# Down projection of a transformer block: all block sums moved from GpSimd to VectorE, the seven products in another order

## The chip, the cores and the metric

One core of one Trainium2 chip. The metric is the device time of one execution in microseconds (us); each kernel is executed several times and the median counts. A profile is one further execution, recorded instruction by instruction.

## What is computed

One layer of a hybrid block over 16 learned tokens and 1024 frames, everything in float32: a combined projection, attention and pooling side by side, an output projection, and then the part that matters here, the gated feed-forward:

```python
n2 = _rmsnorm(h, norm2_w)
ffn = (jax.nn.silu(n2 @ w_gate) * (n2 @ w_up)) @ w_down     # D_MODEL 1024, D_FF 2816
return h + ffn                                              # the 16 learned tokens are dropped at the end
```

The change touches the last product alone, `(...) @ w_down`, with the sum `h + ffn` behind it.

## The kernel before

The kernel runs in stages one after the other: input projections, attention, output projection, gate and up products, down projection. A list written out by hand, not a scheduler, sets the order on each engine: each engine executes its instructions in the order of the program, and waits where an operand or a buffer isn't ready.

**The down projection** is one matrix product: 1024 output rows by 1024 frames, summed over 2816 hidden rows. Hidden rows are stored as 22 tiles of 128 rows, `hid[0..21]`, read back from DRAM; even tiles are called `ha`, odd ones `hc`. The product is done with a scheme of seven block products in place of eight (Strassen's, in Winograd's form): the weights are cut into 2x2 blocks (even or odd hidden tile by lower or upper 512 output rows, `LO` and `HI`), the hidden values into 2x2 blocks (even or odd tile by lower or upper 512 frames). Each of the seven products `j` multiplies one block, or a sum of blocks, of the weights with one block, or a sum, of the hidden values. The outputs are sums of products. `SEQD` (L990) is the order of the products, 1, 2, 4, 6, 7, 5, 3.

**One product** has 11 steps `i` (`NPR`, one for each pair of hidden tiles), so the down projection has 77 steps, numbered x. A step has a weight tile `wd` and a hidden tile `hd`. float32 is multiplied as a rounded part and a remainder, both in a faster format: the tile's lower half holds the rounded values, the upper half the remainders. For each of four output tiles `m` a step issues three matmuls of 128x128 by 128x512 (L1362 to L1364): 12 a step, 132 a product, 924 in all. The four outputs of a product are four PSUM banks; two products' banks fit.

**What a step needs first**, in `d_prep` (L1022):
- the block sum of the weights and that of the hidden values, where the product has one: L1032, L1035, L1041, L1046, L1050, L1054 and L1062 on GpSimd (`G`), L1036 and L1042 on VectorE (`V`);
- for `wd` and then for `hd`: ScalarE casts the values to the rounded part (L1058), VectorE subtracts it from the values to get the remainder (L1059).

So a step's chain is sum, cast, remainder, matmul. `d_ahead(x)` runs ahead of the matmuls of step x: it issues hidden loads up to step x + `HL`, weight loads up to x + `LL` and `d_prep` up to x + `LS` = x + 2 (L1065). All loads are on SyncE's queue (SP), which issues in order.

**The evacuation** `d_evac` (L1330) takes the outputs of a product out of PSUM: one bank m after each of the next product's first four steps, always behind that step's `d_ahead`. Product 1 and product 4 are copied by ScalarE, the others are added by VectorE, straight from PSUM, into `dx`, `du` or `res` tiles (all by the helper at L1325, so they share a line); GpSimd adds `dp` and `du` for one output block (also L1325). `res_load` (L1316) fetches the residual h, which GpSimd adds at step 6 of products 2, 6, 5 and 3. `give` stores a finished output block from ScalarE's queue. In the last product the last three steps (`TL`) are done output by output, so that outputs finish one after the other.

**Buffers**: `ut` tiles (41 of 128x1024) hold the hidden tiles, `wd`, `hd`, `dx`, `du`, `dp` and the stored sums `T2d` and `S2d`; `hs` (10 of 128x512) hold 512-column weights and residuals; `aux` (3 of 128x1024) the wider weight loads.

Of the kernel before, what the change touches and what calls it, by code (L numbers as in the profile page):

```python
# [7 lines left out]
FT = mybir.dt.float32  # L8
FR = mybir.dt.float32r
AF = mybir.ActivationFunctionType  # L10
OP = mybir.AluOpType
# [20 lines left out]
NB = (3, 6)  # L32
CW, KW, SW, W1 = 2, 2, 3, 3
TL = 3
HL, LL, LS = 8, 4, 2
LA = 3
MAXN = {0: (2, 0, 0), 1: (0, 2, 2, 2, 2, 2, 2)}
SUBV = 4
# [7 lines left out]
def block_kernel(ctx, tc, hT, n1w, w_f, w_v, w_u, w_qk, b_f, qnw, knw, w_pool, pscale, w_out, n2w, w_g, w_up, w_d, outT):  # L46
# [12 lines left out]
    def ut(cols, dt=FT, s="u"):  # L59
        return U.tile([128, cols], dt, tag="u", bufs=NU, padded_shape=None, name=nm(s))  # L60
# [14 lines left out]
    V, A, G = nc.vector, nc.scalar, nc.gpsimd  # L75
# [55 lines left out]
    def load(src, cols, mk, eng=None):  # L131
        t = mk(cols, FT, "wst")
        (eng or nc.sync).dma_start(t, src)
        return t

    def aux(cols, dt=FT, s="ax"):
        return U.tile([128, cols], dt, tag="aux", bufs=NAUX, name=nm(s))
# [849 lines left out]

    SEQD = (1, 2, 4, 6, 7, 5, 3)  # L990
    dseq = [(j, i) for j in SEQD for i in range(NPR)]
    horder = [2 * i for i in range(NPR)] + [2 * i + 1 for i in range(NPR)]
    hid, T2d, S2d, wraw, dparts = {}, {}, {}, {}, {}
    dnext = [0, 0, 0]
    LO, HI = slice(0, 512), slice(512, 1024)

# [5 lines left out]

    def d_load(j, i):
        e, o = w_d[2 * i], w_d[2 * i + 1]
        if j in (1, 2, 4, 3):
            return load({1: e[:, LO], 2: o[:, LO], 4: o[:, HI], 3: o[:, LO]}[j], 512, hs)
        if j == 6:
            return load(e, 1024, aux), load(o[:, HI], 512, hs)
        if j == 7:
            return load(e, 1024, aux)  # L1010
        t = aux(1024, FT, "wst")
        nc.sync.dma_start(t[:, LO], e[:, HI])  # L1012
        nc.sync.dma_start(t[:, HI], o[:, HI])
        return t

    def halves(store, i, s):

        if i % 2 == 0:
            store[i // 2] = ut(1024, FT, s)
        return store[i // 2][:, 512 * (i % 2):512 * (i % 2) + 512]  # L1020

    def d_prep(j, i):  # L1022
        w = wraw.pop((j, i))
        ha, hc = hid[2 * i], hid.get(2 * i + 1)

        def t2():
            return T2d[i // 2][:, 512 * (i % 2):512 * (i % 2) + 512]
        if j == 1:
            b = ha[:, LO]
        elif j == 2:  # L1030
            b = hc[:, LO]
            G.tensor_tensor(halves(T2d, i, "T2d"), hc[:, HI], ha[:, LO], op=OP.subtract)  # L1032
        elif j == 4:
            b = hc[:, LO]
            G.tensor_tensor(b, b, t2(), op=OP.subtract)  # L1035
            V.tensor_tensor(ha[:, HI], hc[:, HI], ha[:, HI], op=OP.subtract)  # L1036
        elif j == 6:
            b = t2()
            w, c = w
            s2 = halves(S2d, i, "S2d")  # L1040
            G.tensor_tensor(c, c, w[:, HI], op=OP.add)  # L1041
            V.tensor_tensor(s2, c, w[:, LO], op=OP.subtract)  # L1042
            w = s2
        elif j == 7:
            b = ha[:, HI]
            G.tensor_tensor(w[:, LO], w[:, LO], w[:, HI], op=OP.subtract)  # L1046
            w = w[:, LO]
        elif j == 5:
            b = ha[:, LO]
            G.tensor_tensor(w[:, LO], w[:, LO], w[:, HI], op=OP.add)  # L1050
            w = w[:, LO]
        else:
            b = hc[:, HI]
            G.tensor_tensor(w, w, S2d[i // 2][:, 512 * (i % 2):512 * (i % 2) + 512], op=OP.subtract)  # L1054
        out = []
        for src, name in ((w, "wd"), (b, "hd")):
            t = ut(1024, FR, name)
            A.activation(t[:, LO], src, AF.Copy)  # L1058
            V.tensor_tensor(t[:, HI], src, f(t)[:, LO], op=OP.subtract)  # L1059
            out.append(t)  # L1060
        if j == 1:
            G.tensor_tensor(ha[:, LO], ha[:, HI], ha[:, LO], op=OP.subtract)  # L1062
        dparts[j, i] = out

    def d_ahead(x):  # L1065
# [242 lines left out]
    stores()  # L1308


    ux, uu, up4, todo = [ut(1024, FT, "dx") for _ in range(2)], [], [], []

    def of(ts, m):
        return ts[m // 2][:, 512 * (m % 2):512 * (m % 2) + 512]

    def res_load(r, b):  # L1316
        out = []
        for m in range(4):
            t = hs(512, FT, "res")
            nc.sync.dma_start(t, h2d[4 * r + m][:, 512 * b:512 * b + 512])  # L1320
            out.append(t)
        return out

    def add(e, out, p, q):
        e.tensor_tensor(out, p, q, op=OP.add)  # L1325

    def give(r, b, m, t):
        todo.append(lambda: A.dma_start(outT[4 * r + m][:, 512 * b:512 * b + 512], t))

    def d_evac(j, m, p):  # L1330
        x = of(ux, m)
        if j == 1:
            A.activation(x, p, AF.Copy)
        elif j == 2:
            t = res.pop(0)
            add(V, t, p, t)
            give(0, 0, m, t)
        elif j == 4:
            A.activation(of(up4, m), p, AF.Copy)
        elif j == 6:  # L1340
            add(V, x, p, x)
        elif j == 7:
            u, t = of(uu, m), of(up4, m)
            add(V, u, p, x)
            add(G, t, t, u)
            give(1, 0, m, t)
        elif j == 5:
            t = res.pop(0)
            add(V, t, p, t)
            add(V, x, p, x)  # L1350
            give(1, 1, m, t)


    RES = {2: (0, 0, lambda m: of(ux, m)), 6: (1, 0, lambda m: of(up4, m)), 5: (1, 1, lambda m: of(uu, m)),
           3: (0, 1, lambda m: of(ux, m))}
    res, done = [], []

    def part(j, steps, m, p):
# [5 lines left out]
            mm(p, w[:, W], h[:, HI], start=False, stop=i == NPR - 1)  # L1364

    for y, j in enumerate(SEQD):
        if j == 4:
            up4.extend(ut(1024, FT, "dp4") for _ in range(2))
        if j == 7:
            uu.extend(ut(1024, FT, "du") for _ in range(2))  # L1370
        pb = [ps("d") for _ in range(4)]
        tl = TL if j == SEQD[-1] else 0
        for i in range(NPR - tl):
            d_ahead(NPR * y + i)
            for m in range(4):
                part(j, (i,), m, pb[m])
            dparts.pop((j, i))
            while todo:
                todo.pop(0)()
            if done:  # L1380
                d_evac(*done.pop(0))
            elif j in RES and i == 4:
                r, b, with_ = RES[j]
                res.extend(res_load(r, b))
            elif j in RES and i == 6:
                for m in range(4):
                    t = RES[j][2](m)
                    if j == 6:
                        add(G, t, t, res.pop(0))
                    else:  # L1390
                        add(G, res[m], res[m], t)
        if not tl:
            done.extend((j, m, pb[m]) for m in range(4))
    d_ahead(len(dseq) - 1)
# [1 line left out]
        todo.pop(0)()  # L1396
    for m in range(4):
        part(j, range(NPR - tl, NPR), m, pb[m])
        t = res.pop(0)
        add(V, t, pb[m], t)  # L1400
        A.dma_start(outT[m][:, HI], t)

# [51 lines left out]
```

## Time and profile before

| | us |
|---|---|
| median of 3 runs | 1186.5 (1186.46 to 1186.7) |
| profiled execution, its own time | 1182.54 |
| its span, first to last instruction | 1180.8 |
| TensorE busy in the span | 1131.0 (96%) |
| VectorE busy | 786.7 (67%) |
| GpSimd busy | 566.8 (48%) |
| ScalarE busy | 483.7 (41%) |

The profiled execution is 4.0 us under the median of the runs, and 1.7 us over its own span. "Busy" counts an instruction from its start to its end; matmuls follow each other before the one in front has ended, so a busy TensorE can still run slowly, and how fast it runs is read from the distance of two matmuls' starts. The granted clock is given as a share of TensorE's full 2.4 GHz.

### The profile page before, as it was taken

How to read it: one execution, taken by the hardware profiler on the slowest of the kernel's cores; microseconds unless marked ns; L12 is line 12 of the kernel's file. 1: busy time of each engine (PE TensorE's matmuls, PEld its weight loads, DVE VectorE, ACT ScalarE, POOL GpSimd, SP SyncE). 2: the span in 40 equal slices, each digit the busy share in tenths (PEclk: the TensorE clock that was granted, in tenths of full speed). 3: DMA queues.
4: the chain of work that ended last, by engine and by line, in shares of the span. 5: the costliest groups of instructions: out<-in, count | busy, mean ns of one | idle time of the engine just before them, and what ended most of it. 6: DMA issues, size and time to landing. Idle time of an engine off the chain costs nothing. (4 is left out here: it accounts for less than half of the span.)

```text
span 1180.8 us, 14713 instructions
## 1 busy us (share of the span) xinstructions
PE 1131.0 (96%) x5251; PEld 922.5 (78%) x5251; DVE 786.7 (67%) x1144; ACT 483.7 (41%) x903; POOL 566.8 (48%) x433
## 2 busy tenths in 40 slices
PE   6899999999999999898999999999999998999988
PEld 5787999787888878676888888888888886767766
DVE  7524753774888877899455545544555599988587
ACT  7333421532788775434333123322332362334332
POOL 6200235142446574647435533453345389465493
PEclk9899999999999999998999999999999999999989
DMA  6201110251021131221223221323132692566554
GB/s 218 72 1 54 36 54 10 64 162 45 19 48 34 29 110 75 100 79 57 82 76 105 74 84 59 107 72 102 42 107 74 240 372 72 180 222 195 171 170 132
DMA packets 49993, 118.23 MB, mean 100 GB/s; under 512 B 6736, under 2 KB 9296, under 8 KB 49920
## 3 DMA queue, kind: packets, MB, share of 16 engines
q1 hardware_dynamic: 40096, 101.00, 26.2%
q10 hardware_dynamic: 9824, 16.30, 3.7%
q8 instruction: 41, 0.67, 0.2%
q14 instruction: 32, 0.26, 0.1%
HBM read 91.86 MB, written 19.92 MB: 95 GB/s over the span
## 5 line engine op out<-in xcount | busy, mean ns | idle before, releaser
L1124 PE MATMUL gu<-cb,ws 128*128 128x512 f32 x560 | 221.7, 396 | 4.1 <-DVE ws L1114 4.1
L1125 PE MATMUL gu<-cb,ws 128*128 128x512 f32 x560 | 221.6, 396 | 0.0
L1123 PE MATMUL gu<-cb,ws 128*128 128x512 f32 x560 | 221.2, 395 | 0.0
L1114 DVE TENSOR_TENSOR ws<-wst,ws 128x512 fp32r<-128x512 f32 x120 | 97.2, 810 | 125.1 <-ACT ws L1113 125.0
L1364 PE MATMUL d<-hd,wd 128*128 128x512 f32 x308 | 125.9, 409 | 8.2 <-DVE hd L1059 7.6
L1124 PEld LDWEIGHTS gu<-cb,ws 128*128 128x128 f32 x560 | 105.8, 189 | 29.6 <-DVE ws L1114 4.5
L1362 PE MATMUL d<-hd,wd 128*128 128x512 f32 x308 | 123.8, 402 | 4.0 <-ACT hd L1058 3.9
L1113 ACT ACTIVATE ws<-wst 128x512 fp32r<-128x512 f32 x120 | 69.9, 621 | 138.8 <-POOL wst L1108 130.9
L1125 PEld LDWEIGHTS gu<-cb,ws 128*128 128x128 f32 x560 | 105.9, 189 | 24.6
L1363 PE MATMUL d<-hd,wd 128*128 128x512 f32 x308 | 123.8, 402 | 1.4 <-DVE wd L1059 1.3
L1123 PEld LDWEIGHTS gu<-cb,ws 128*128 128x128 f32 x560 | 105.7, 189 | 24.7
L1137 POOL TENSOR_TENSOR e<-e,e 128x512 f32<-128x512 f32 x20 | 29.6, 1478 | 159.5 <-DVE e L1150 99.8
L1059 DVE TENSOR_TENSOR wd<-wst,wd 128x512 fp32r<-128x512 f32 x66 | 70.2, 1063 | 25.6 <-ACT wd L1058 25.5
L1058 ACT ACTIVATE wd<-wst 128x512 fp32r<-128x512 f32 x66 | 41.6, 630 | 108.5 <-POOL wst L1050 27.8
L293 POOL TENSOR_TENSOR s<-t,g 128x346 f32<-128x346 f32 (+2 forms) x20 | 21.5, 1081 | 131.9 <-ACT g L292 121.2
L1059 DVE TENSOR_TENSOR hd<-wst,hd 128x512 fp32r<-128x512 f32 x66 | 84.6, 1282 | 0.0
L736 POOL TENSOR_TENSOR pl<-p,ph 128x512 fp32r<-128x512 f32 (+4 forms) x58 | 64.8, 1130 | 41.1 <-ACT p L728 38.5
L1364 PEld LDWEIGHTS d<-hd,wd 128*128 128x128 f32 x308 | 59.1, 192 | 29.6 <-DVE hd L1059 16.8
L1362 PEld LDWEIGHTS d<-hd,wd 128*128 128x128 f32 x308 | 59.3, 192 | 18.3 <-ACT hd L1058 5.7
L402 PE MATMUL pj<-xh,wl 128*128 128x346 f32 (+2 forms) x216 | 72.9, 338 | 0.0
L401 PE MATMUL pj<-xh,wh 128*128 128x346 f32 (+2 forms) x216 | 72.9, 337 | 0.0
L403 PE MATMUL pj<-xl,wh 128*128 128x346 f32 (+2 forms) x216 | 72.9, 337 | 0.0
(296 smaller groups left out, 2694.5 us busy)
## 6 DMA issues: line engine op xcount, KB each, us to landing
wst<-in_w_d SPq DMA_DIRECT2D x77, 256.0 KB, 4.6
wst<-in_w_g SPq DMA_DIRECT2D x22, 512.0 KB, 4.8
wst<-in_w_up SPq DMA_DIRECT2D x22, 512.0 KB, 3.5
wst<-hidd SPq DMA_DIRECT2D x22, 512.0 KB, 3.8
wst<-in_w_d SPq DMA_DIRECT2D x22, 512.0 KB, 4.4
hidd<-e ACTq DMA_DIRECT2D x20, 256.0 KB
h<-in_hT SPq DMA_DIRECT2D x8, 512.0 KB, 7.5
h2d<-h SPq DMA_DIRECT2D x16, 256.0 KB, 2.0
```

Source lines behind the costliest of these rows:

```text
L401: mm(p[:, :n], wh[:, W], xh[k][:, o:o + n], start=k == 0, stop=False)
L402: mm(p[:, :n], wl[:, W], xh[k][:, o:o + n], start=False, stop=False)
L403: mm(p[:, :n], wh[:, W], xl[k][:, o:o + n], start=False, stop=k == KT - 1)
L1059: V.tensor_tensor(t[:, HI], src, f(t)[:, LO], op=OP.subtract)
L1113: A.activation(t[:, :512], src, AF.Copy)
L1114: E.tensor_tensor(t[:, 512:], src, f(t)[:, :512], op=OP.subtract)
L1123: mm(p, w[:, W], c[:, :512], start=k == 0, stop=False)
L1124: mm(p, w[:, Wl], c[:, :512], start=False, stop=False)
L1125: mm(p, w[:, W], c[:, 512:], start=False, stop=k == 3)
L1362: mm(p, w[:, W], h[:, LO], start=i == 0, stop=False)
L1363: mm(p, w[:, Wl], h[:, LO], start=False, stop=False)
L1364: mm(p, w[:, W], h[:, HI], start=False, stop=i == NPR - 1)
```

## The change

- The products are done in the order 1, 2, 5, 6, 4, 7, 3, and weights are loaded five steps ahead, not four (`LL`).
- Every block sum of the down projection is done by VectorE (`sub`), 88 in all, where GpSimd did 77 before and VectorE 22; GpSimd has no instruction left in the down projection. Each sum replaces one of its own terms: `S12` holds the weights' sum of product 5, from which those of products 6 and 3 are made in place; the hidden sums replace halves of `ha` and `hc`. `T2d`, `S2d` and `du` are gone.
- Product 6's second weight block is no longer loaded with it: its 512 lower columns of the even tile are loaded alone, so that a step of it needs one load of 256 KB.
- The sums of the outputs are all on VectorE: the residual for output block (0, 1) is loaded in product 6 and serves as the accumulator to the end (`last`); product 5 is copied from PSUM by ScalarE; product 6's evacuation has three VectorE additions for each bank, so has product 7's. Residuals are added at steps 7 to 10 of products 2, 4 and 7, one a step.

```diff
-HL, LL, LS = 8, 4, 2
+HL, LL, LS = 8, 5, 2
...
-    SEQD = (1, 2, 4, 6, 7, 5, 3)
+    SEQD = (1, 2, 5, 6, 4, 7, 3)
...
     def d_load(j, i):
         e, o = w_d[2 * i], w_d[2 * i + 1]
-        if j in (1, 2, 4, 3):
-            return load({1: e[:, LO], 2: o[:, LO], 4: o[:, HI], 3: o[:, LO]}[j], 512, hs)
-        if j == 6:
-            return load(e, 1024, aux), load(o[:, HI], 512, hs)
         if j == 7:
             return load(e, 1024, aux)
+        if j != 5:
+            return load({1: e[:, LO], 2: o[:, LO], 6: e[:, LO], 4: o[:, HI], 3: o[:, LO]}[j], 512, hs)
         t = aux(1024, FT, "wst")
...
+        if j == 5 and i % 2 == 0:
+            S12[i // 2] = ut(1024, FT, "S12")
+        sc = S12[i // 2][:, 512 * (i % 2):512 * (i % 2) + 512] if i // 2 in S12 else None
+
+        def sub(out, p, q, op=OP.subtract):
+            V.tensor_tensor(out, p, q, op=op)
+            return out
         if j == 1:
             b = ha[:, LO]
         elif j == 2:
             b = hc[:, LO]
-            G.tensor_tensor(halves(T2d, i, "T2d"), hc[:, HI], ha[:, LO], op=OP.subtract)
+        elif j == 5:
+            b = ha[:, LO]
+            w = sub(sc, w[:, LO], w[:, HI], OP.add)
+        elif j == 6:
+            w = sub(sc, sc, w)
+            b = sub(ha[:, LO], hc[:, HI], ha[:, LO])
         elif j == 4:
-            b = hc[:, LO]
-            G.tensor_tensor(b, b, t2(), op=OP.subtract)
-            V.tensor_tensor(ha[:, HI], hc[:, HI], ha[:, HI], op=OP.subtract)
-        elif j == 6:
-            b = t2()
-            w, c = w
-            s2 = halves(S2d, i, "S2d")
-            G.tensor_tensor(c, c, w[:, HI], op=OP.add)
-            V.tensor_tensor(s2, c, w[:, LO], op=OP.subtract)
-            w = s2
+            b = sub(hc[:, LO], hc[:, LO], ha[:, LO])
         elif j == 7:
             b = ha[:, HI]
-            G.tensor_tensor(w[:, LO], w[:, LO], w[:, HI], op=OP.subtract)
-            w = w[:, LO]
-        elif j == 5:
-            b = ha[:, LO]
-            G.tensor_tensor(w[:, LO], w[:, LO], w[:, HI], op=OP.add)
-            w = w[:, LO]
+            w = sub(w[:, LO], w[:, LO], w[:, HI])
         else:
             b = hc[:, HI]
-            G.tensor_tensor(w, w, S2d[i // 2][:, 512 * (i % 2):512 * (i % 2) + 512], op=OP.subtract)
+            w = sub(sc, w, sc)
...
         if j == 1:
-            G.tensor_tensor(ha[:, LO], ha[:, HI], ha[:, LO], op=OP.subtract)
+            sub(ha[:, LO], ha[:, HI], ha[:, LO])
+        elif j == 2:
+            sub(ha[:, HI], hc[:, HI], ha[:, HI])
...
+        elif j == 5:
+            A.activation(of(up5, m), p, AF.Copy)
         elif j == 4:
             A.activation(of(up4, m), p, AF.Copy)
         elif j == 6:
             add(V, x, p, x)
+            t = res.pop(0)
+            add(V, t, t, x)
+            add(V, t, t, of(up5, m))
+            last.append(t)
         elif j == 7:
-            u, t = of(uu, m), of(up4, m)
-            add(V, u, p, x)
-            add(G, t, t, u)
-            give(1, 0, m, t)
-        elif j == 5:
-            t = res.pop(0)
-            add(V, t, p, t)
+            t5, t4 = of(up5, m), of(up4, m)
             add(V, x, p, x)
-            give(1, 1, m, t)
+            add(V, t4, t4, x)
+            add(V, t5, t5, x)
+            give(1, 0, m, t4)
+            give(1, 1, m, t5)
...
-            elif j in RES and i == 4:
-                r, b, with_ = RES[j]
-                res.extend(res_load(r, b))
-            elif j in RES and i == 6:
-                for m in range(4):
-                    t = RES[j][2](m)
-                    if j == 6:
-                        add(G, t, t, res.pop(0))
-                    else:
-                        add(G, res[m], res[m], t)
+            elif j in RES and i == (6 if j == 4 else 4):
+                res.extend(res_load(*RES[j][:2]))
+            elif j in RES and RES[j][2] and 7 <= i < 11:
+                m, t = i - 7, RES[j][2](i - 7)
+                if j == 2:
+                    add(V, res[m], res[m], t)
+                else:
+                    add(V, t, t, res.pop(0))
```

The change moves instructions between two engines. Three places show how. In the changed kernel the sums stand at L1023, the remainders at L1047 and the additions to outputs at L1315; `wst` is a loaded weight tile or a hidden tile, `S_...` an `S12` tile, `d_...` a PSUM bank.

GpSimd before, at the end of product 5 (the residual's additions at its step 6, then the weights' sums of products 5 and 3):

```order
L1325 TENSOR_TENSOR res_9569<-res_9569,du_9195 128x512
L1325 TENSOR_TENSOR res_9571<-res_9571,du_9195 128x512
L1050 TENSOR_TENSOR wst_9573<-wst_9573 128x512
L1050 TENSOR_TENSOR wst_9595<-wst_9595 128x512
L1054 TENSOR_TENSOR wst_9621<-wst_9621,S2d_8870 128x512
```

VectorE in the changed kernel, at steps 7 and 8 of product 7, where the same kinds of work stand:

```order
L1023 TENSOR_TENSOR wst_9517<-wst_9517 128x512
L1047 TENSOR_TENSOR wd_9591<-wst_9517,wd_9591 128x512
L1047 TENSOR_TENSOR hd_9594<-wst_8178,hd_9594 128x512
L1315 TENSOR_TENSOR dp_9164<-dp_9164,res_9538 128x512
L1023 TENSOR_TENSOR wst_9546<-wst_9546 128x512
L1047 TENSOR_TENSOR wd_9613<-wst_9546,wd_9613 128x512
L1047 TENSOR_TENSOR hd_9616<-wst_8201,hd_9616 128x512
L1315 TENSOR_TENSOR dp_9164<-dp_9164,res_9540 128x512
```

What was a queue of its own now stands between the remainders, one sum ahead of each pair, and one residual's addition behind a pair.

VectorE before, where the last product (3) begins and the banks of product 5 are evacuated:

```order
L1059 TENSOR_TENSOR wd_9712<-wst_9663,wd_9712 128x512
L1059 TENSOR_TENSOR hd_9715<-wst_8268,hd_9715 128x512
L1325 TENSOR_TENSOR res_9565<-d_9439,res_9565 128x512
L1325 TENSOR_TENSOR dx_8135<-d_9439,dx_8135 128x512
L1059 TENSOR_TENSOR wd_9735<-wst_9684,wd_9735 128x512
L1059 TENSOR_TENSOR hd_9738<-wst_8291,hd_9738 128x512
```

VectorE in the changed kernel at the same place, with the banks of product 7:

```order
L1023 TENSOR_TENSOR S_1608_8659<-wst_9610,S_1608_8659 128x512
L1047 TENSOR_TENSOR wd_9683<-S_1608_8659,wd_9683 128x512
L1047 TENSOR_TENSOR hd_9686<-wst_8270,hd_9686 128x512
L1315 TENSOR_TENSOR dx_8137<-d_9425,dx_8137 128x512
L1315 TENSOR_TENSOR dp_9164<-dp_9164,dx_8137 128x512
L1315 TENSOR_TENSOR dp_8650<-dp_8650,dx_8137 128x512
L1023 TENSOR_TENSOR S_1608_8659<-wst_9632,S_1608_8659 128x512
L1047 TENSOR_TENSOR wd_9707<-S_1608_8659,wd_9707 128x512
L1047 TENSOR_TENSOR hd_9710<-wst_8293,hd_9710 128x512
```

Between two pairs of remainders stood two additions; now three additions and a sum stand there. The first addition reads the bank that product 7's last step fills, and the steps behind it queue behind it.

VectorE in the changed kernel where product 4 begins and the banks of product 6 are evacuated:

```order
L1023 TENSOR_TENSOR wst_8270<-wst_8270,wst_8041 128x512
L1047 TENSOR_TENSOR wd_9173<-wst_9100,wd_9173 128x512
L1047 TENSOR_TENSOR hd_9176<-wst_8270,hd_9176 128x512
L1315 TENSOR_TENSOR dx_8137<-d_8908,dx_8137 128x512
L1315 TENSOR_TENSOR res_9026<-res_9026,dx_8137 128x512
L1315 TENSOR_TENSOR res_9026<-res_9026,dp_8650 128x512
L1023 TENSOR_TENSOR wst_8293<-wst_8293,wst_8060 128x512
L1047 TENSOR_TENSOR wd_9197<-wst_9122,wd_9197 128x512
L1047 TENSOR_TENSOR hd_9200<-wst_8293,hd_9200 128x512
```

Here the sum (first row) is that of the hidden values, which the third row needs and the second doesn't; each of the three additions reads what the one in front of it wrote.

## Rows read from the trace of the kernel before

**Rows 1.** By product: stretch, length, each engine's busy us (instructions), PEclk, DMA share, GB/s.
```profile
936.01:966.78 30.77, 30.77 (x133) 24.73 (x132) 26.97 (x26) 14.22 (x26) 22.53 (x15) 1.00 0.93 350
966.78:999.95 33.17, 31.75 (x134) 24.39 (x132) 33.17 (x20) 13.81 (x25) 33.17 (x20) 1.00 0.37 131
999.95:1035.01 35.06, 32.86 (x133) 25.57 (x132) 32.21 (x43) 10.16 (x18) 18.98 (x9) 0.95 0.52 175
1035.01:1073.13 38.12, 34.69 (x133) 25.50 (x132) 30.19 (x29) 14.51 (x26) 21.49 (x15) 0.96 0.58 199
1073.13:1103.99 30.86, 30.77 (x133) 24.72 (x132) 25.11 (x29) 13.14 (x23) 18.64 (x12) 1.00 0.63 204
1103.99:1145.10 41.11, 35.43 (x134) 26.27 (x133) 25.78 (x24) 14.57 (x26) 30.75 (x21) 0.92 0.54 179
1145.10:1176.88 31.78, 31.09 (x133) 24.46 (x131) 26.44 (x32) 7.97 (x14) 15.63 (x11) 1.00 0.40 128
```
The engines stand in the order TensorE, its weight loads, VectorE, ScalarE, GpSimd; the products in the order 1, 2, 4, 6, 7, 5, 3.

**Rows 2.** Timeline of TensorE (start, us, line): two matmuls with 174 between them.
```profile
1008.45 0.39 PE L1364 MATMUL d<-hd,wd 128*128 128x512 f32 x1
...
1048.86 0.39 PE L1362 MATMUL d<-hd,wd 128*128 128x512 f32 x1
```

**Rows 3.** Waits of TensorE and VectorE, down projection: total us, times, longest.
```profile
PE d L1364 <- DVE hd L1059: 7.6, 14, 1.2
PE d L1362 <- ACT hd L1058: 3.9, 3, 1.8
PE d L1363 <- DVE wd L1059: 1.3, 3, 0.6
...
DVE wd L1059 <- ACT wd L1058: 34.0, 23, 3.8
```

**Rows 4.** Timeline of VectorE and of GpSimd in product 2.
```profile
990.58 1.77 DVE L1059 TENSOR_TENSOR wd<-wst,wd 128x512 fp32r<-128x512 f32 x1
992.27 1.79 DVE L1059 TENSOR_TENSOR hd<-wst,hd 128x512 fp32r<-128x512 f32 x1
...
988.37 10.24 POOL L1035 TENSOR_TENSOR wst<-wst,T2d 128x512 f32<-128x512 f32 x6
```

**Rows 5.** Timeline of VectorE while GpSimd is idle (start of product 7).
```profile
1073.72 0.68 DVE L1059 TENSOR_TENSOR wd<-wst,wd 128x512 fp32r<-128x512 f32 x1
1074.32 0.68 DVE L1059 TENSOR_TENSOR hd<-wst,hd 128x512 fp32r<-128x512 f32 x1
```

**Rows 6.** Timeline of VectorE and ScalarE, a step of product 6, sum on VectorE.
```profile
1046.01 0.68 DVE L1042 TENSOR_TENSOR S2d<-wst,wst 128x512 f32<-128x512 f32 x1
...
1046.78 0.63 ACT L1058 ACTIVATE wd<-S2d 128x512 fp32r<-128x512 f32 x1 [1.92 <-DVE S2d L1042]
...
1047.45 0.69 DVE L1059 TENSOR_TENSOR wd<-S2d,wd 128x512 fp32r<-128x512 f32 x1 [0.76 <-ACT wd L1058]
...
1048.06 1.79 DVE L1059 TENSOR_TENSOR hd<-T2d,hd 128x512 fp32r<-128x512 f32 x1
```

**Rows 7.** Timeline of VectorE: the second subtraction reads the first one's result.
```profile
522.33 0.69 DVE L1201 TENSOR_TENSOR h<-h 128x512 f32<-128x512 f32 x1
523.05 1.67 DVE L1203 TENSOR_TENSOR T<-h,h 128x512 f32<-128x512 f32 x1
```

**Rows 8.** Timeline of TensorE: a matmul that waited, and two of those behind it.
```profile
1002.58 0.51 PE L1364 MATMUL d<-hd,wd 128*128 128x512 f32 x1 [1.18 <-DVE hd L1059]
...
1004.86 0.63 PE L1362 MATMUL d<-hd,wd 128*128 128x512 f32 x1
1005.28 0.63 PE L1363 MATMUL d<-hd,wd 128*128 128x512 f32 x1
```

**Rows 9.** DMA issues: KB each, median us from issue to landing.
```profile
wst<-in_w_d SPq DMA_DIRECT2D x22, 512.0 KB, 4.4
h<-in_hT SPq DMA_DIRECT2D x8, 512.0 KB, 7.5
```

More of the change, by code (lines that the diff above doesn't have):

```diff
@@ L985, in block_kernel @@
             stream += [(i, u, j) for j in SEQ7 if i > PRE or j > 2]
-    SEQD = (1, 2, 4, 6, 7, 5, 3)
+    SEQD = (1, 2, 5, 6, 4, 7, 3)
     dseq = [(j, i) for j in SEQD for i in range(NPR)]
     horder = [2 * i for i in range(NPR)] + [2 * i + 1 for i in range(NPR)]
-    hid, T2d, S2d, wraw, dparts = {}, {}, {}, {}, {}
+    hid, S12, wraw, dparts = {}, {}, {}, {}
     dnext = [0, 0, 0]
@@ L1014, in d_load @@
         return t
[L1016 to L1020, printed above, removed]
     def d_prep(j, i):
@@ L1024, in d_prep @@
         ha, hc = hid[2 * i], hid.get(2 * i + 1)
-        def t2():
-            return T2d[i // 2][:, 512 * (i % 2):512 * (i % 2) + 512]
+        if j == 5 and i % 2 == 0:
[4 more added lines that the diff above has]
+            return out
         if j == 1:
@@ L1308, in block_kernel @@
     stores()
-    ux, uu, up4, todo = [ut(1024, FT, "dx") for _ in range(2)], [], [], []
+    ux, up5, up4, todo = [ut(1024, FT, "dx") for _ in range(2)], [], [], []
     def of(ts, m):
@@ L1341, in d_evac @@
             add(V, x, p, x)
+            t = res.pop(0)
+            add(V, t, t, x)
+            add(V, t, t, of(up5, m))
+            last.append(t)
         elif j == 7:
-            u, t = of(uu, m), of(up4, m)
-            add(V, u, p, x)
-            add(G, t, t, u)
-            give(1, 0, m, t)
-        elif j == 5:
-            t = res.pop(0)
-            add(V, t, p, t)
-            add(V, x, p, x)
-            give(1, 1, m, t)
-    RES = {2: (0, 0, lambda m: of(ux, m)), 6: (1, 0, lambda m: of(up4, m)), 5: (1, 1, lambda m: of(uu, m)),
-           3: (0, 1, lambda m: of(ux, m))}
+            t5, t4 = of(up5, m), of(up4, m)
+            add(V, x, p, x)
+            add(V, t4, t4, x)
+            add(V, t5, t5, x)
+            give(1, 0, m, t4)
+            give(1, 1, m, t5)
+    RES = {2: (0, 0, lambda m: of(ux, m)), 6: (0, 1, None), 4: (1, 1, lambda m: of(up5, m)),
+           7: (1, 0, lambda m: of(up4, m))}
+    last = []
     res, done = [], []
@@ L1366, in block_kernel @@
     for y, j in enumerate(SEQD):
[L1367 to L1370, printed above, removed]
+        if j in (5, 4):
+            (up5 if j == 5 else up4).extend(ut(1024, FT, "dp") for _ in range(2))
         pb = [ps("d") for _ in range(4)]
@@ L1398, in block_kernel @@
         part(j, range(NPR - tl, NPR), m, pb[m])
-        t = res.pop(0)
+        t = last[m]
         add(V, t, pb[m], t)
```

## The prediction

> **What bounds the kernel now.** I read the page first (TensorE is busy 96% of the span, so it sets the time), then the down projection by product, then what TensorE waits for there, then single instructions. A busy TensorE tells little by itself: two matmul starts with 174 matmuls between them lie 40.41 us apart [rows 2], which is 0.231 us for each. A step of 12 matmuls then needs 2.77 us, a product of 132 needs 30.5 us, all seven 213.4 us. They took 240.9 us [rows 1]: **27.5 us are lost**, by product 0.3, 2.7, 4.6, 7.6, 0.4, 10.6 and 1.3 us in the order 1, 2, 4, 6, 7, 5, 3. TensorE's own idle time there is only 12.8 us [rows 3], because the view counts a matmul as busy until its late end; the starts count. Part of the loss is a lower clock: behind a wait that ends at 1002.58 matmuls start 0.42 us apart [rows 8], and the product has a mean granted clock of 0.95 where undisturbed ones have 1.00 [rows 1]: some of it at 1.2 GHz, the rest at 2.4. In the trace 25 matmuls start 0.41 to 0.44 us apart like these, some 25 x 0.2 = 5 us of the 27.5; the rest is waiting for remainders and casts [rows 3].
>
> Why are they late? With GpSimd idle, a remainder takes 0.68 us and the next starts 0.60 us after it [rows 5]. While GpSimd adds without a pause, one takes 1.77 us and they start 1.70 us apart, in step with GpSimd's 10.24 / 6 = 1.71 us for each of its own [rows 4]. One instruction of either engine then passes at a time. In product 2 both engines are busy for all of its 33.17 us with 20 instructions each, and TensorE is late [rows 1]. A transfer isn't the cause: product 1 has the highest DMA share, 0.93, and loses 0.3 us [rows 1].
>
> **The change, part by part.** *GpSimd's 97 instructions leave the down projection* (77 sums, 20 additions). No VectorE instruction is held up there any more, and each is priced at its undisturbed pitch of 0.60 us, or 0.72 us where the next one reads its result [rows 7]. *VectorE gets 86 more:* 88 sums for 22, and 44 additions for 24.
>
> What a step costs VectorE now follows from the chain. Where the weights' sum comes first (products 5, 7, 3), sum to cast is 0.77 us, cast to remainder 0.67, to the second remainder 0.61, to the next sum 0.60 [rows 6, 5]: **2.65 us a step, 0.8 us of it VectorE waiting for ScalarE's cast.** Nothing fills that wait, since the engine works in order and the remainder stands next. Product 6 has two sums, but the second fits into the wait: 2.65 us again. Product 4's sum is that of the hidden values, and the weights' remainder fits into the wait: 0.77 + 0.67 + 0.60 = 2.04. Products 1 and 2 have their sums behind the remainders: 3 x 0.60 = 1.8. TensorE needs 2.77 a step.
>
> *Products 1 and 2:* 1.8 of 2.77 us; the loss of product 2 goes, the 0.3 of product 1 (its start, not VectorE's) stays. *Products 5 and 6:* 2.65 of 2.77, a margin of 0.12 us a step. Product 2's four evacuating additions cost 2.4 us at the start of product 5, but at that moment three steps are ready (`d_ahead` stands ahead of the evacuation), 8.3 us of cover. Product 5 is copied by ScalarE. No stall.
>
> *Products 4, 7 and 3* are where it is no longer hidden. From the first addition of product 6's bank, VectorE has, without a pause:
> - product 6's evacuation, 4 x (0.72 + 0.72 + 0.60) = 8.2 us;
> - eight steps of product 4 (three are ready), 8 x 2.04 = 16.3;
> - 22 steps of products 7 and 3, 22 x 2.65 = 58.3;
> - eight residual additions, 8 x 0.60 = 4.8;
> - product 7's evacuation, 4 x (0.72 + 0.60 + 0.60) = 7.7.
>
> Sum 95.3 us. It begins when the first of product 6's banks is done, 9 matmuls or 2.1 us ahead of that product's end, plus 0.2 us, by which a matmul's end (0.39) lies behind the next one's start (0.23) [rows 2]. The last remainder's end lies 0.1 us behind its pitch [rows 5]. Behind it TensorE still has 28 matmuls (the last three steps go output by output, so the last step is needed early), 6.5 us. Together 95.3 - 2.1 + 0.2 + 0.1 + 6.5 = 100.0 us for three products that TensorE alone does in 91.4: **a new loss of 8.6 us**, nearly all in the last product, from its fourth step on. I take 1.5 us more for a lowered clock behind those waits; it lies between nothing (a slow matmul inside a wait costs nothing) and 28 x 0.20 = 5.6 us.
>
> *Other edits.* 22 loads of 256 KB fewer and one more step ahead: nothing, TensorE waits for no load in [rows 3]. ScalarE's four more copies: nothing, it is busy 14.6 us at most in a product [rows 1]. VectorE's queue has behind the evacuating addition all later steps, and that is in the list; the stores on ScalarE's queue wait for additions that VectorE has done ahead of the next cast's sum, so they hold up nothing. Products 5 and 7 have three buffers for their wide loads: buffer free, load, next sum is 0.77 + 0.67 + 0.69 + 4.4 = 6.5 us [rows 6, 9] for three steps of 2.65 = 8.0: covered by 1.5 us, and what a longer landing costs is a rival below.
>
> **Sum.** Lost before 27.5; after 8.6 + 1.5 + 0.3 = 10.4; gain 17.1 us. The profiled execution goes from 1182.5 to 1165.4. The median of the runs lies 4.0 us above it now and I keep that distance: **1169.4 us**. Its own bounds: 0.05 us less on 30 steps and no clock loss gives 3 us more gain (1166.4); 0.1 us more on 30 steps, 5.6 us of clock and 2 us of late loads give 9.1 less (1178.5).
>
> **One rule weighed.** [Rows 5] show VectorE starting an instruction 0.60 us after the last, ahead of its end at 0.68. The Trainium skill, "VectorE: DVE Perf Modes", section "The DRAIN you can't avoid", has the next instruction start only when the pipeline has emptied, though another section of that page lets one start earlier that isn't held. By [rows 5] the new loss is 8.6 us; with starts 0.69 us apart it would be 8.6 + 72 x 0.09 = 15.1 us (72 of the 122 instructions of the list are not followed by a wait).
>
> **Rivals.**
> - *Everything is hidden* (7%): VectorE doesn't wait for the cast, so a step costs 1.8 us, the list is 22 x 0.8 = 18 us shorter, and all but 0.3 us of the loss goes: 1159.3. Against it: 23 waits of VectorE for that cast stand in [rows 3], and [rows 6] shows one.
> - *VectorE's starts lie a full instruction apart* (6%), 0.69 in place of 0.60 us, as if each waited for the end of the one in front. Loss 8.6 + 72 x 0.09 + 1.8 = 16.9: 1175.9. For it [rows 7], against it [rows 5].
> - *The stretching isn't GpSimd's doing, or not alone* (7%, and slower): transfers landing in the same tiles, or ScalarE's reads, stretch VectorE too. Place: the same three products, then also 5 and 6, whose margin is 0.12. If p is the pitch, the list grows by 72 (p - 0.60), products 5 and 6 by 44 (p - 0.60) - 2.6, of which some 3 us are covered. At p = 0.80 the loss is 8.6 + 14.4 + 3.2 + 1.8 = 28, what it was, and from there on it is slower; at 1.0 it is 8.6 + 28.8 + 12 + 1.8 = 51 us: 1210. Against it: [rows 5], and product 1 with the fullest DMA and no loss [rows 1]. That the change frees nothing ends here too.
> - *The ring of three wide buffers sets the pace* (4%): with landings of 7.5 us, the longest of that size [rows 9], in place of 4.4, product 7's step is (2.1 + 7.5) / 3 = 3.2 us, 11 x 0.55 = 6 us more: 1175.5. Four times that would be needed to be slower.
>
> **How the numbers follow.** The forecast has 74%, the four rivals 24%; 2% are left for what I don't see. The range 1164 to 1179 holds the forecast's bounds, the full-pitch and ring cases, and leaves out the hidden and the stretched case, 14%. A measurement of this kernel tells 0.2%, 2.4 us, from no change. Faster are forecast, hidden, full pitch and ring, 91%, of which I take off 3 for waits on VectorE's longer queue that add up to the whole gain: 0.88. These 3 and the 2 unseen are the case of no change: 0.05. Slower: 0.07.
>
> **What would show it.** In the profile after, no GpSimd row in the down projection; remainders at a mean of 0.68 to 0.70 us, none at 1.77 as in [rows 4]; products 1, 2, 5, 6, 4, 7 each 30.5 to 31.5 us long at full clock; product 3 some 40 us, with waits on the remainders from its fourth step; waits of VectorE on the cast of 0.8 us in most steps of products 5, 7 and 3. Wrong would be: waits already in products 5 or 6, remainders above 0.8 us, or TensorE waiting on loads.

## The result and the profile after

The changed kernel takes **1168.92 us** (median of 4 runs, 1168.05 to 1170.24) against 1186.55 us before (4 runs, 1186.46 to 1186.7): a ratio of **0.9852, 95% interval 0.9835 to 0.9869**, 17.6 us less. The prediction was 1169.4 us, with 1164 to 1179 as the range.

The profiled execution took 1168.22 us:

| | before | after |
|---|---|---|
| span, us | 1180.8 | 1166.4 |
| TensorE busy | 1131.0 | 1122.6 |
| VectorE busy | 786.7 | 764.6 |
| GpSimd busy | 566.8 | 405.7 |
| ScalarE busy | 483.7 | 487.1 |

VectorE has 86 instructions more in the down projection and is yet busy for 22 us less. The down projection by product, in the new order 1, 2, 5, 6, 4, 7, 3 (columns as in [rows 1]):

```profile
939.75:970.38 30.63, 30.63 (x133) 24.80 (x132) 25.11 (x41) 14.16 (x26) 2.55 (x2) 1.00 0.94 347
970.38:1000.92 30.54, 30.54 (x133) 24.82 (x132) 23.18 (x38) 12.75 (x25) 0.00 (x0) 1.00 0.55 198
1000.92:1031.38 30.46, 30.46 (x133) 24.81 (x132) 24.71 (x40) 12.96 (x23) 0.00 (x0) 1.00 0.75 233
1031.38:1061.96 30.58, 30.58 (x133) 24.82 (x132) 26.55 (x43) 15.40 (x26) 0.00 (x0) 1.00 0.29 95
1061.96:1092.49 30.53, 30.53 (x134) 24.80 (x133) 27.46 (x44) 11.03 (x19) 0.00 (x0) 1.00 0.36 121
1092.49:1122.88 30.39, 30.39 (x133) 24.80 (x132) 22.33 (x37) 14.39 (x26) 0.00 (x0) 1.00 0.62 204
1122.88:1162.55 39.67, 33.53 (x133) 24.20 (x131) 28.36 (x45) 10.60 (x19) 0.00 (x0) 1.00 0.30 106
```

Six products now take the 30.5 us that TensorE needs alone (132 matmuls at 0.231 us are 30.48); all that is lost, 9.2 us, lies in the last one, at full clock. The sum is 222.8 us against 240.9: **18.1 us less**. The span fell by only 14.4 us, since the attention stage, which the change doesn't touch, took less time in the profiled execution of the kernel before: 172.9 us from its first to its last score matmul (L659), against 176.7 in this one and 175.9 to 178.5 in the seven that follow. The down projection began at 936.0 there and at 939.75 here, 3.7 us later; why, no run tells. The two instructions of GpSimd in the first row still belong to the stage in front.

VectorE's groups in the down projection, grouped by form (busy us, mean ns of one, idle us before them and what ended it), where [rows 4] had 1.77 us:

```profile
L1047 DVE TENSOR_TENSOR hd<-wst,hd 128x512 fp32r<-128x512 f32 x77 | 52.9, 687 | 4.1 <-ACT hd L1046 4.1
L1047 DVE TENSOR_TENSOR wd<-wst,wd 128x512 fp32r<-128x512 f32 x44 | 31.0, 705 | 13.2 <-ACT wd L1046 13.2
L1047 DVE TENSOR_TENSOR wd<-S,wd 128x512 fp32r<-128x512 f32 x33 | 22.9, 693 | 18.1 <-ACT wd L1046 17.8
```

The waits there, which answer to [rows 3]:

```profile
DVE wd L1047 <- ACT wd L1046: 30.9, 43, 3.2
...
PE d L1356 <- ACT hd L1046: 5.8, 5, 1.3
```

TensorE waited 14 times for remainders of the hidden values before; now five long waits end with the cast `hd`. VectorE waits 43 times for the cast `wd`, in 41 of them for the cast of a sum that it made itself; the other two, the longest among them, lie in products 1 and 2, which have no such sum. The mean of 705 ns for `wd` has one remainder of 1.46 us in it (935.61), beside GpSimd's work for the stage in front; behind that all remainders take 0.68 or 0.69 us. VectorE's timeline (start, us; in brackets the idle time ahead and what ended it) shows the two ends of the list on which the forecast loss rests, a step of product 7, and a step of product 3 with an evacuation:

```profile
1060.08 0.69 DVE L1047 TENSOR_TENSOR hd<-wst,hd 128x512 fp32r<-128x512 f32 x1 [0.89 <-ACT hd L1046]
1060.69 0.69 DVE L1315 TENSOR_TENSOR dx<-d,dx 128x512 f32<-128x512 f32 x1
...
1098.31 0.68 DVE L1023 TENSOR_TENSOR wst<-wst 128x512 f32<-128x512 f32 x1
1099.75 0.69 DVE L1047 TENSOR_TENSOR wd<-wst,wd 128x512 fp32r<-128x512 f32 x1 [0.75 <-ACT wd L1046]
1100.36 0.68 DVE L1047 TENSOR_TENSOR hd<-wst,hd 128x512 fp32r<-128x512 f32 x1
1100.96 0.69 DVE L1023 TENSOR_TENSOR wst<-wst 128x512 f32<-128x512 f32 x1
...
1131.03 0.69 DVE L1047 TENSOR_TENSOR hd<-wst,hd 128x512 fp32r<-128x512 f32 x1
1131.63 0.68 DVE L1315 TENSOR_TENSOR dx<-d,dx 128x512 f32<-128x512 f32 x1
1132.35 1.29 DVE L1315 TENSOR_TENSOR dp<-dp,dx 128x512 f32<-128x512 f32 x2
1133.56 0.69 DVE L1023 TENSOR_TENSOR S<-wst,S 128x512 f32<-128x512 f32 x1
1135.00 0.69 DVE L1047 TENSOR_TENSOR wd<-S,wd 128x512 fp32r<-128x512 f32 x1 [0.76 <-ACT wd L1046]
1135.61 0.69 DVE L1047 TENSOR_TENSOR hd<-wst,hd 128x512 fp32r<-128x512 f32 x1
...
1155.21 0.68 DVE L1047 TENSOR_TENSOR hd<-wst,hd 128x512 fp32r<-128x512 f32 x1
```

In product 7 it is 2.65 us from sum to sum (1098.31 to 1100.96), 0.75 of it idle. In product 3 the step is 1135.61 - 1131.03 = 4.58 us long, where TensorE needs 2.77. ScalarE's and TensorE's timelines at the same place:

```profile
1134.34 0.63 ACT L1046 ACTIVATE wd<-S 128x512 fp32r<-128x512 f32 x1 [3.43 <-DVE S L1023]
...
1134.87 0.61 ACT L1046 ACTIVATE hd<-wst 128x512 fp32r<-128x512 f32 x1
```

```profile
1133.97 0.40 PE L1358 MATMUL d<-hd,wd 128*128 128x512 f32 x1
1135.54 0.51 PE L1356 MATMUL d<-hd,wd 128*128 128x512 f32 x1 [1.18 <-ACT hd L1046]
...
1136.35 0.51 PE L1358 MATMUL d<-hd,wd 128*128 128x512 f32 x1
```

The cast `hd` needs no sum in product 3; it stands behind the cast `wd` on ScalarE, which waits for VectorE's sum. It ends at 1135.48, and the step's first matmul starts at 1135.54, 1.57 us after the last one of the step in front. The step's third matmul then waits once more, for the remainder of the hidden values (1135.61 + 0.69 = 1136.30), and starts at 1136.35: of the step's two waits the one for the remainder ends last.

### The profile page after: what moved, and what is told of

Read it like the earlier page. It is cut to its first block, busy times and chain, and to the rows that moved or that the text cites. A ratio compares the mean times of both kernels' runs of the same rounds, so it can differ in the third digit from the quotient of the medians.

```text
span 1166.4 us, 14589 instructions
## 1 busy us (share of the span) xinstructions
PE 1122.6 (96%) x5251; PEld 920.6 (79%) x5251; DVE 764.6 (66%) x1230; ACT 487.1 (42%) x907; POOL 405.7 (35%) x336
## 4 chain that ended last, share of the span: by engine, by line
PE 80%; DVE 13%; ACT 4%; issue 2%; DMA 0%; ACTq 0%; POOL 0%; SPq 0%; DVEq 0%; POOLq 0%
PE gu L1114 11%; PE gu L1115 11%; PE gu L1113 11%; PE d L1358 5%; PE d L1356 5%; PE d L1357 5%; PE pj L402 3%; PE pj L401 3%; PE pj L403 3%; PE o L500 2%; PE o L501 2%; PE o L502 2%; PE v L240 2%; PE v L242 1%; PE v L241 1%
## 5 line engine op out<-in xcount | busy, mean ns | idle before, releaser
L1356 PE MATMUL d<-hd,wd 128*128 128x512 f32 x308 | 121.7, 395 | 5.8 <-ACT hd L1046 5.8
L1358 PE MATMUL d<-hd,wd 128*128 128x512 f32 x308 | 121.9, 396 | 0.4
L1357 PE MATMUL d<-hd,wd 128*128 128x512 f32 x308 | 121.1, 393 | 0.0
L1356 PEld LDWEIGHTS d<-hd,wd 128*128 128x128 f32 x308 | 57.9, 188 | 20.7 <-ACT hd L1046 7.8
L1358 PEld LDWEIGHTS d<-hd,wd 128*128 128x128 f32 x308 | 57.9, 188 | 15.6 <-DVE hd L1047 2.5
L1357 PEld LDWEIGHTS d<-hd,wd 128*128 128x128 f32 x308 | 57.9, 188 | 13.3
L1046 ACT ACTIVATE hd<-wst 128x512 fp32r<-128x512 f32 x77 | 48.0, 623 | 21.4 <-DVE wst L1023 16.2
L1047 DVE TENSOR_TENSOR hd<-wst,hd 128x512 fp32r<-128x512 f32 x77 | 52.9, 687 | 4.1 <-ACT hd L1046 4.1
```

Source lines behind the costliest of these rows:

```text
L1356: mm(p, w[:, W], h[:, LO], start=i == 0, stop=False)
L1357: mm(p, w[:, Wl], h[:, LO], start=False, stop=False)
```

## The experiments

Two theories stood at the start. **A:** before, GpSimd's instructions held VectorE's up; the gain is that they are gone, and what is lost now is VectorE's wait for ScalarE's cast of its own sum. **B:** the new order, the sums in place and the fewer loads have a share of their own. Rivals to A's first half: any work of GpSimd, or transfers, stretch VectorE. Loss by product in each profiled execution (its stretch less 30.48 us), worked out from the windows by product:

| kernel | 1 | 2 | 4 | 5 | 6 | 7 | 3 | all |
|---|---|---|---|---|---|---|---|---|
| before | 0.3 | 2.7 | 4.6 | 10.6 | 7.6 | 0.4 | 1.3 | 27.5 |
| after | 0.2 | 0.1 | 0.1 | 0.0 | 0.1 | -0.1 | 9.2 | 9.4 |
| e1, old order, all on VectorE | 0.2 | 0.0 | -0.1 | 5.9 | 1.2 | 1.3 | 12.0 | 20.5 |
| e2, 33 sums on GpSimd | 0.2 | 0.1 | 0.1 | 0.0 | 0.0 | -0.1 | 6.1 | 6.3 |
| e3, loads four steps ahead | 0.2 | 0.1 | -0.1 | -0.1 | 0.0 | 0.1 | 12.0 | 12.0 |
| e4, sums one step ahead | 0.2 | 0.1 | 0.0 | 0.1 | -0.1 | 0.0 | 0.1 | 0.3 |
| e5, idle GpSimd reads | 11.4 | 11.1 | 1.7 | 0.8 | 0.1 | -0.1 | 13.0 | 37.9 |
| e6, idle GpSimd writes | 0.2 | 0.1 | 0.1 | 0.0 | 0.1 | -0.1 | 10.7 | 11.0 |
| e7, e1 with sums ahead | 0.1 | 0.0 | 0.0 | 0.0 | 0.1 | -0.2 | 0.0 | 0.1 |

**e1: the engine alone.** The kernel before, with its order, buffers and loads; only the engine of its sums and additions is changed (ten lines like these):

```diff
-            G.tensor_tensor(b, b, t2(), op=OP.subtract)
+            V.tensor_tensor(b, b, t2(), op=OP.subtract)
...
-            add(G, t, t, u)
+            add(V, t, t, u)
```

> The kernel before with one edit: every block sum, residual addition and output addition of the down projection on VectorE. Order of the products, loads and buffers stay as before. If GpSimd's instructions holding VectorE up is what was lost: the losses of product 2 (2.7 us) and product 4 (4.6) go to under 0.5 us each, no VectorE row at 1.77 us. VectorE's own list is then the bound from product 6 on, where the two weight sums read one another (0.72 + 0.77 + 0.67 + 0.61 + 0.60 = 3.37 us a step against TensorE's 2.77): 11 x 3.37 + 22 x 2.65 and 19 us of additions, a loss of 13 to 18 us in products 6, 7, 5 and 3, in all about 1176 us (1173 to 1179). If the new order, the fewer loads or the in-place buffers bring the gain: 1186 or slower, with the losses of products 2 and 4 where they were.

1179.47 us (4 runs, 1178.15 to 1182.08), ratio 0.9939 (0.9921 to 0.9957). The losses of products 2 and 4 are gone, as A has it: GpSimd no longer holds the remainders up. But the total is 20.5 us, and the time lies just above the expected range. VectorE's list is longer than after's, as expected, since product 6 has two sums, one reading the other; 2.4 us of a lowered clock in product 3 (see e6) come on top. Its timeline, one step:

```profile
1041.30 0.68 DVE L1041 TENSOR_TENSOR wst<-wst,wst 128x512 f32<-128x512 f32 x1
1042.09 0.69 DVE L1042 TENSOR_TENSOR S2d<-wst,wst 128x512 f32<-128x512 f32 x1
1043.48 0.69 DVE L1059 TENSOR_TENSOR wd<-S2d,wd 128x512 fp32r<-128x512 f32 x1 [0.70 <-ACT wd L1058]
...
1044.69 0.69 DVE L1041 TENSOR_TENSOR wst<-wst,wst 128x512 f32<-128x512 f32 x1
```

3.39 us a step against TensorE's 2.77 and against 2.65 in the changed kernel; then 7, 5 and 3 follow with the cast's wait in every step. Moving the engine alone is worth 27.5 - 20.5 = 7 us of the 18; the rest needs the change's shorter list. By this run B's parts count, as long as VectorE's list is the bound.

**e2: the weights' sums of 5, 7 and 3 back on GpSimd**, the rest as changed (33 sums, which then could run beside VectorE):

```diff
-            w = sub(w[:, LO], w[:, LO], w[:, HI])
+            w = sub(w[:, LO], w[:, LO], w[:, HI], e=G)
...
-            w = sub(sc, w, sc)
+            w = sub(sc, w, sc, e=G)
```

> The changed kernel with the 33 weight sums of products 5, 7 and 3 back on GpSimd, all else as changed. If VectorE's list is the bound and a GpSimd instruction costs VectorE only the 1.1 us for which it holds up one instruction: a step is 2 x 0.60 + 1.1 = 2.3 us in place of 2.65, since VectorE no longer waits for the cast of its own sum; the list is 22 x 0.35 = 7.7 us shorter and product 3 loses 1 to 3 us in place of 9.2: 1161 to 1164 us. If it takes a GpSimd-free down projection to be fast: losses come back in products 5, 7 and 3, 1172 to 1180 us.

1167.29 us (1165.85 to 1168.57), ratio 0.9833 (0.9818 to 0.9848): neither number, and in time not told from the changed kernel, whose interval overlaps. In products 5 and 7 nothing is lost, in product 3 6.1 us. GpSimd's timeline shows why, in product 7 and from its end on:

```profile
1109.44 1.81 POOL L1023 TENSOR_TENSOR wst<-wst 128x512 f32<-128x512 f32 x1 [1.33 <-DMA wst<-in_w_d]
1112.51 1.29 POOL L1023 TENSOR_TENSOR wst<-wst 128x512 f32<-128x512 f32 x1 [1.26 <-DMA wst<-in_w_d]
...
1117.66 18.27 POOL L1023 TENSOR_TENSOR S<-wst,S 128x512 f32<-128x512 f32 x11
```

In product 7 it idles ahead of its sums, in most cases until a load lands in one of the three wide buffers: about one sum a step. For product 3 the loads go to ten narrow buffers, and it does all eleven without a pause. VectorE's timeline, first at the two sums of product 7, then in that stretch, which is [rows 4] again:

```profile
1109.41 0.69 DVE L1047 TENSOR_TENSOR hd<-wst,hd 128x512 fp32r<-128x512 f32 x1
...
1112.55 1.80 DVE L1047 TENSOR_TENSOR hd<-wst,hd 128x512 fp32r<-128x512 f32 x1
...
1126.25 1.78 DVE L1315 TENSOR_TENSOR dp<-dp,res 128x512 f32<-128x512 f32 x1
1127.95 1.78 DVE L1047 TENSOR_TENSOR wd<-S,wd 128x512 fp32r<-128x512 f32 x1
```

So a GpSimd sum costs little where something paces it, and holds VectorE up where nothing does: A's first half, shown inside one kernel.

**e3: loads four steps ahead**, as before the change, in the changed kernel:

```diff
-HL, LL, LS = 8, 5, 2
+HL, LL, LS = 8, 4, 2
```

> The changed kernel with weight loads four steps ahead, as before, in place of five. If loads bound nothing: 1169 within 1.5 us, product 3 again at some 9 us of loss. If the fifth step is needed: TensorE or VectorE waits for weight loads in products 5 or 7, 1171 or more.

1170.61 us (1168.87 to 1171.02), ratio 0.9859 (0.9844 to 0.9873); the interval overlaps the changed kernel's, so in time it isn't told from it. The profile shows one late load in product 7, which the changed kernel doesn't have:

```profile
1112.54 0.69 DVE L1023 TENSOR_TENSOR wst<-wst 128x512 f32<-128x512 f32 x1 [1.41 <-DMA wst<-in_w_d]
```

It delays VectorE's list by 1.4 us, and product 3 loses 2.8 us more than after; how the rest comes about stands under e6.

**e4: the sums one step ahead of the remainders**, all else as changed. `d_prep` is cut in two: `d_sum` (the block sums) runs up to step x + 3, casts and remainders up to x + 2 as they did, so that on VectorE the next step's sum stands ahead of this step's remainders:

```diff
+        while dnext[3] < len(dseq) and dnext[3] <= x + LS + 1:
+            d_sum(*dseq[dnext[3]])
+            dnext[3] += 1
         while dnext[1] < len(dseq) and dnext[1] <= x + LS:
             d_prep(*dseq[dnext[1]])
```

> The changed kernel with each step's sums issued one step further ahead, so that the next step's sum stands in VectorE's queue ahead of this step's remainders. The number of VectorE instructions is the same. If the wait for the cast makes the list too long: a step is 3 x 0.60 = 1.8 us (2.4 in product 6), the list of the last three products is some 20 us shorter, product 3 loses under 1 us, and the time is 1169 - 9 = 1160 us (1158.5 to 1162). If the number of VectorE instructions is what counts: 1169, with product 3 at 39 to 40 us.

**1159.47 us** (1158.24 to 1162.36), ratio 0.9771 (0.9755 to 0.9787): below the changed kernel's interval, and 27 us below before. The windows' last row (product 3) and sum, and VectorE's timeline in that product's preparation:

```profile
1121.84:1152.42 30.58, 30.58 (x133) 24.65 (x131) 21.79 (x36) 8.08 (x14) 0.00 (x0) 1.00 0.27 99
sum 213.66, PE 213.66 PEld 173.59 DVE 174.44 ACT 90.66 POOL 2.55; mean PE 30.52 PEld 24.80 DVE 24.92 ACT 12.95 POOL 0.36
```

```profile
1115.69 0.69 DVE L1025 TENSOR_TENSOR S<-wst,S 128x512 f32<-128x512 f32 x1
1116.30 0.69 DVE L1057 TENSOR_TENSOR wd<-S,wd 128x512 fp32r<-128x512 f32 x1
1116.90 0.69 DVE L1057 TENSOR_TENSOR hd<-wst,hd 128x512 fp32r<-128x512 f32 x1
1117.50 0.69 DVE L1328 TENSOR_TENSOR dp<-dp,res 128x512 f32<-128x512 f32 x1
```

No wait stands between them: four instructions start within 2.4 us, where the changed kernel's step of 2.65 and an addition take 3.2. VectorE's waits for the cast `wd`, 30.9 us in 43 times in the changed kernel, are down to:

```profile
DVE wd L1057 <- ACT wd L1056: 7.3, 3, 3.2
```

The instructions are the same in number and kind; with the wait for the cast went the whole 9.2 us.

**e5 and e6: GpSimd work that nobody needs**, 44 instructions added to the changed kernel in its first steps: in e5 subtractions of a tile from itself (they read SBUF twice), in e6 fills of the same tile (they only write):

```diff
+            if NPR * y + i < 44:
+                G.tensor_tensor(maskB, maskB, maskB, op=OP.subtract)
```

```diff
+            if NPR * y + i < 44:
+                G.memset(maskB, 0.0)
```

> The changed kernel with 44 GpSimd subtractions added on a 128x512 tile that nothing reads any more (it holds the attention's mask), one put into the program at each of the first 44 steps. Nothing holds them back, so GpSimd runs them in a row from the start of the down projection. If GpSimd's instructions as such hold VectorE up: for some 75 us (44 x 1.7) VectorE's instructions take 1.77 us and start 1.70 us apart, 44 of them in the time in which products 1, 2 and 5 need 81; those products lose 15 to 30 us together: 1185 to 1200 us. If it was data that GpSimd shared with the other engines, or waits on its results: nothing reads these, 1169 us.

> The changed kernel with 44 GpSimd memsets of the same tile in place of those subtractions: they write and read nothing. If GpSimd holds VectorE up only while it reads: VectorE's instructions stay at 0.68 to 0.70 us, 1169 us. If any GpSimd instruction does: VectorE's rows of 1.1 us or more as long as the memsets run (44 x 0.6 = 25 us alone, longer if they are held up themselves), and a loss of some us in product 1.

e5 took 1196.72 us, e6 1169.95 (one run each; before on the same chip 1185.96). Both ran their 44 without a pause. GpSimd and VectorE in e5:

```profile
945.60 63.48 POOL L1368 TENSOR_TENSOR maskB<-maskB 128x512 f32<-128x512 f32 x44
```

```profile
950.22 1.52 DVE L1047 TENSOR_TENSOR wd<-wst,wd 128x512 fp32r<-128x512 f32 x1
951.67 1.52 DVE L1047 TENSOR_TENSOR hd<-wst,hd 128x512 fp32r<-128x512 f32 x1
```

and in e6:

```profile
945.80 25.67 POOL L1368 MEMSET maskB<- 128x512 f32 x44
```

```profile
950.80 0.69 DVE L1047 TENSOR_TENSOR wd<-wst,wd 128x512 fp32r<-128x512 f32 x1
951.40 0.69 DVE L1047 TENSOR_TENSOR hd<-wst,hd 128x512 fp32r<-128x512 f32 x1
```

63.48 / 44 = 1.44 us apart on GpSimd, and 1.45 on VectorE, one for one; products 1 and 2, where nothing was lost, lose 11 us each. With fills VectorE keeps 0.60. The stretching is GpSimd's doing, and it takes reads. The Trainium skill, "SBUF — State Buffer", section "Who interferes with whom", says the same: a VectorE instruction with two SBUF inputs contends with a GpSimd instruction that reads SBUF, not with one that only writes it; both rows agree.

e6 also shows what the clock costs. Its product 3 loses 1.5 us more than the changed kernel's, though VectorE's list takes 95.2 us in both. Its timeline of TensorE behind a wait in the last three steps:

```profile
1155.45 0.50 PE L1356 MATMUL d<-hd,wd 128*128 128x512 f32 x1 [1.28 <-ACT hd L1046]
...
1156.86 0.63 PE L1356 MATMUL d<-hd,wd 128*128 128x512 f32 x1
1157.28 0.63 PE L1357 MATMUL d<-hd,wd 128*128 128x512 f32 x1
```

Matmuls 0.42 us apart, as in [rows 8]; the product's mean granted clock is 0.96. e1, e2, e3 and e5 have 6 to 12 such matmuls in product 3 too, each 0.2 us longer than at full clock; the changed kernel's profiled execution has none. In e3 product 3 ends 7.75 us behind VectorE's last remainder and in the changed kernel 6.66, which is 1.1 of its 2.8 us; the other 1.7 are a longer list on VectorE, 1.4 of it the late load. In e5 VectorE reaches the first addition to product 6's banks 2.0 us behind the end of that product (1087.11), in the changed kernel 1.3 us ahead of it: these 3.3 us, 0.6 of a longer list and 1.5 of a lowered clock are the 5.5 us that products 4, 7 and 3 lose more in e5. That VectorE was still behind there from its stretched instructions fits the little room that products 5 and 6 leave it (0.12 us a step), but no run shows it by itself.

**e7: the old order with the sums ahead.** e1 with e4's step: old order, loads and buffers, all on VectorE, sums one step ahead.

```diff
-            G.tensor_tensor(b, b, t2(), op=OP.subtract)
+            V.tensor_tensor(b, b, t2(), op=OP.subtract)
...
+        while dnext[3] < len(dseq) and dnext[3] <= x + LS + 1:
+            d_sum(*dseq[dnext[3]])
+            dnext[3] += 1
```

> The kernel before with all sums and additions on VectorE (as in the first experiment) and each step's sums issued one step further ahead; order, loads and buffers stay as before. A step is 1.8 us in products 7, 5 and 3, 2.4 in product 4 and 2.5 in product 6. If VectorE's list with its waits for the cast is all that is left: the loss of 20.5 us falls under 2, 1160 to 1162 us. If the new order, the in-place sums or the fewer loads have a share: 1164 us or more, with a loss in product 6, whose steps load 768 KB, or in product 3.

**1159.16 us** (1158.77 to 1162.47), ratio 0.9787 (0.9762 to 0.9812), not to be told from e4. Its windows' sum:

```profile
sum 213.43, PE 213.43 PEld 173.35 DVE 181.29 ACT 90.30 POOL 2.55; mean PE 30.49 PEld 24.76 DVE 25.90 ACT 12.90 POOL 0.36
```

So B falls where the wait is filled: order, sums in place and fewer loads are worth 11 us (20.5 - 9.4, 2.4 of it e1's lowered clock) while VectorE's list is the bound, and nothing once it isn't. e4 and e7 beat both kernels, and with 213.4 to 213.7 us TensorE has nothing left to wait for in this stage. Not tried: the sums one step ahead but left on GpSimd, GpSimd's sums spread out by hand in product 3, and what the attention stage's 3.7 us are.

## Why the prediction was right, point by point

- **What bound the kernel before** (GpSimd's instructions hold VectorE's up): right. The remainders went from 1.77 to 0.69 us; e2 brings the stretch back where GpSimd runs without a pause, e5 makes it with work that has nothing to do with the step, e6 shows that writes don't.
- **Products 1, 2, 5, 6, 4, 7 hidden:** right, 30.39 to 30.63 us each, at full clock. The margin of 0.12 us a step in products 5 and 6 held.
- **VectorE's list of 95.3 us:** it runs from 1060.69 to 1155.21 + 0.68, 95.2 us. Its parts: step of product 4 2.07 us (2.04 forecast), step of product 7 2.59 to 2.65 (2.65), a bank of product 7's evacuation 1.93 (1.92).
- **New loss 8.6 us in the last product, from its fourth step:** 9.2, with the first wait of over 1 us behind the fourth step (1135.54). Mis-sized by 0.6: the list began 1.3 us ahead of product 6's end, not 1.9. In front of the first addition stood a remainder of the hidden values that had waited 0.89 us for its cast (1060.08), which the sum of the list left out.
- **1.5 us for a lowered clock:** not in this execution, where product 3 has a clock of 1.00. Where it came, the size was near: 6 to 8 matmuls and 1.1 to 1.5 us in e2, e3, e5 and e6, 12 and 2.4 us in e1.
- **Which wait ends last:** I named the remainders, and in each late step the wait for the remainder of the hidden values does end last (1136.35). What I didn't name is the longer wait in front of it, for the cast `hd`, held behind the cast `wd` on ScalarE: 5.8 us of TensorE's idle time are put down to it. Both hang on the same VectorE sum.
- **Sum:** 10.4 us lost by forecast, 9.4 measured; gain 17.1 forecast, 18.1 in the stage. The median fell by 17.6. That the median was hit to 0.5 us is in part luck: a loss mis-sized by 0.6 us and 1.5 us of clock that didn't come have opposite signs. That the profiled execution would keep 4.0 us below the median was wrong (1168.22 against 1168.92): in the one execution before, the attention stage was shorter by about as much. That this is where the distance came from is inferred, since the other runs of that kernel weren't profiled.
- **The rule weighed:** [rows 5] held. In the changed kernel a remainder starts 0.61 us after the one in front, which ends at 0.69 (1099.75 and 1100.36), and the loss is 9.2 us, not 15.1. The Trainium skill, "VectorE: DVE Perf Modes", section "The DRAIN you can't avoid", says that the next instruction does not start until the pipeline has emptied, and adds that one that isn't held starts earlier; the trace agrees with the addition, at 0.61 us, and not with the first half.
- **Rivals:** all hidden fell with the waits on the cast (e4 gets there by another order of issue: 1159.5, the rival had 1159.3); full pitch with the row above; stretching by something else with remainders of 0.68 or 0.69 us throughout the down projection, in product 1 beside a DMA share of 0.94; the ring of three with no wait of VectorE for a load after the change. In e3 one such wait came. (The 7.5 us of that rival are a median in [rows 9], not the longest landing.)
- **Other edits:** the "22 loads of 256 KB fewer" are 11 of 512 KB by the pages of the two profiles (22 of that size before, 11 after, and 77 of 256 KB in both): the same bytes, and e7 has them without loss.
- Of the experiments' expectations, e1's was 2.5 us too low in loss (2.4 us of slow matmuls in product 3 alone), e2's missed on both sides, because neither theory counted what paces GpSimd. e3 lies between its two numbers. e5's time and loss fell into their ranges with VectorE's instructions 1.45 us apart, not the 1.70 expected.

## What to carry to other kernels

When two engines' instructions go one for one, each stretched well over its undisturbed time, taking one engine's work off can make the other faster even if it inherits that work; price the inherited work at the undisturbed pitch, then add up the receiving engine's list in order. In that list look for a wait on another engine's answer to an instruction just issued: issuing the producer one step ahead of the consumers fills the wait with no further instruction, here 9 us, half of the 18 that the whole change brought and more than the 7 of moving the instructions alone. Where the bound is a list, savings in it count; where it isn't, the same savings are worth nothing.

## What the runs showed of the hardware that I had not expected

- GpSimd's fills (0.58 us apart) leave VectorE's instructions at 0.69 us; only its reads hold them up.
- The price of that differs by operands: 1.44 us for a pair of instructions where GpSimd subtracts a tile from itself, 1.70 where it reads two different blocks (e2, and [rows 4]). Why was not tried.
- Of a single pair, the one that starts second waits: in e2 GpSimd's sum of 1109.44, 0.03 us behind a remainder of 0.69, takes 1.81 us; at 1112.51 it comes 0.04 us ahead, takes 1.29, and the remainder 1.80.
- Behind the waits of product 3 TensorE fell to 0.42 us a matmul in the profiled executions of e1, e2, e3, e5 and e6, and not in that of the changed kernel, whose list is e6's: about 1.5 us that one execution has and another hasn't.
